# Norms of the Hyena filters: one channel per partition, and a later place for row 0

## The chip, the cores and the metric

The kernel runs on one core of a Trainium2 chip. The metric is the time of one execution on the device in microseconds (us), as the median of several runs. A core has five engines that work side by side, each through its own queue in order: TensorE (PE: matmuls; PEld is its loading of weights), VectorE (DVE), ScalarE (ACT), GpSimd (POOL) and SyncE (SP), which here only issues transfers.

## The reference, cut to what matters

One encoder block on x of shape (1, 2048, 1024): a projection, a Fourier group and a Hyena group side by side, an output projection, and an MLP. The change lies in the long filters of the Hyena group: 2 orders x 512 channels, each 4096 positions long.

```python
h = (h @ w_out).reshape(l, HYENA_ORDER, N_DIRECTIONS, HYENA_WIDTH)
h = h * decay[:, None, None, :]
k = concatenate([h_fwd[:1] + h_bwd[:1], h_fwd[1:], zeros, h_bwd[1:][::-1]], axis=0)
k = k * rsqrt(sum(k * k, axis=0, keepdims=True) + EPS)      # a norm for every channel
...
k_freq = rfft(k, axis=0)
for n, gate in enumerate((x1, x2)):
    z = gate * (irfft(rfft(z, 2l) * k_freq[:, n])[:l] + z * long_d[n])
```

## The kernel before, in words

The stages follow each other: first projection (two passes), Fourier group with the filters running beside it, rest of the filters, Hyena convolutions, output projection, MLP. The filters are the function `filters`. It works on eight units: `Unit(ct, n)` is a block of 128 channels (`ct` 0 to 3) of one order (`n` 0 or 1); units 0 to 3 are order 0, units 4 to 7 order 1.

A unit goes through these steps:

- `generate(q)`, q = 0 to 7: four matmuls make filter values (positions on partitions), DVE multiplies by a decay that was loaded (L500), ACT rounds to the high part (L181), DVE (even q) or POOL (odd q) subtracts for the low part (L182). For the norm ACT squares (L510) and POOL adds up over q (L511); after q = 7 two more additions (L513, L514) leave one 128 x 128 tile of sums, positions by channels. The squares have a single buffer, so each waits for the addition before it.
- `normalise()`: a matmul of ones with this tile (L518) puts the sum of every channel into all 128 rows. DVE adds EPS, ACT takes the root, DVE the reciprocal and a Newton step (L197 to L208), all on 128 x 128. The filter itself stays unnormalised; the product of the two orders' norms scales v later (L534, L538). So that the skip term `z * long_d` comes out right, long_d divided by the norm is added to the filter's position 0: `dk` is loaded, multiplied and added to the saved row 0 (L526 to L528) on one partition, and rounded and subtracted into row 0 of the high and low parts (L531, L532).
- `stage1(c)`, c = 0 to 7: three matmuls with 512 columns each (high x high, high x low, low x high: L189 to L191), then a DVE transpose into `Gk` (L418). Row 0 is among what it reads, in both parts.
- `stage2(q)`, q = 0 to 7: four matmuls (L553) that read all eight transposes, a copy by ACT (L556), and after every second one a store by SP (L558).

The loop over units runs both stages of unit i, and generates unit i + 2 between them: at the steps of `GENERATE` (3, 5, 7, 7, 9, 11, 13, 15, where steps 0 to 7 are stage 1 and 8 to 15 stage 2). Unit i + 1 is normalised in unit i's second stage, behind q = 1 (in unit 0: behind c = 5 of the first stage). Unit 0 is normalised while unit 1 is generated, beside the Fourier group. In unit 6 the first stage of unit 7 is put between the last steps of the second stage (`LAST`).

The order in every engine's queue is made when the program is built. Program order is the priority; a planner keeps its own clock for each operation, and where the operand of the next one isn't there yet by that clock it puts other, ready work in front. On the chip each queue then runs as laid down. Semaphores and waits are placed by the same framework. Buffers rotate in pools; the results of matmuls take eight banks in turn.

Of the kernel before, what the change touches and what calls it, by code (L numbers as in the profile page):

```python
# [10 lines left out]
F32 = mybir.dt.float32  # L11
# [3 lines left out]
ALU = mybir.AluOpType  # L15

EPS = 1e-5
# [110 lines left out]
P = 128  # L128
# [6 lines left out]
def hybrid_block(ctx: ExitStack, tc: tile.TileContext, A, out):  # L135
    nc = tc.nc
# [25 lines left out]
    def pool(name, side="left"):  # L162
        return tc.tile_pool(name=name, bufs=1, side=side, reuse_waits="tile")

    def pa(nm):
        return ps.tile([P, 512], F32, tag="a", name=nm, bufs=8)
# [304 lines left out]
    def filters(ctx, fp, gp, zp, zzs, norms, emb, wo, e1k, f2):  # L471


        e1h, e1l = (fp.tile([P, P], FR, tag=n, name=n) for n in ("e1h", "e1l"))
        split(e1h, e1l, e1k)

        class Unit:
            def __init__(self, ct, n):
                self.ct, self.n = ct, n

            def generate(self, q):
                if q == 0:

                    i = units.index(self)
                    if i in (1, 4):
                        k = zp.tile([P, 2, 8, 32, 16], FR, tag="zz", name="k")
                        self.k = [k[:, j] for j in range(2)]
                    else:
                        self.k = [(sp if i in (2, 5, 7) else fp).tile([P, 8, 32, 16], FR, tag=n, name=n) for n in ("kh", "kl")]
                    self.acc = fp.tile([P, 4, 128], F32, tag="acc", name="acc", bufs=2)  # L490
                if q % 2 == 0:
                    self.dec = load(fp, "dec", [P, 8, 128], A["decay"][self.ct][:, 4 * q : 4 * q + 8, :], 2)
                dec = self.dec[:, 4 * (q % 2) : 4 * (q % 2) + 4, :]
                p = pa("pk")
                for i in range(4):
                    nc.tensor.matmul(
                        p[:, 128 * i : 128 * i + 128], lhsT=emb[:, 4 * q + i, :], rhs=wo[:, self.n, 128 * self.ct : 128 * self.ct + 128], start=True, stop=True
                    )
                k4 = fp.tile([P, 4, 128], F32, tag="kt", name="kt", bufs=2)
                nc.vector.tensor_mul(k4, p.rearrange("p (l c) -> p l c", l=4), dec)  # L500
                if q == 0:
                    self.k0 = fp.tile([1, 128], F32, tag="k0", name="k0", bufs=2)
                    nc.vector.tensor_copy(self.k0, k4[0:1, 0, :])
                hi, lo = (t.rearrange("p c l j -> p l c j")[:, 4 * q : 4 * q + 4] for t in self.k)
                split(hi, lo, k4.rearrange("p l (c j) -> p l c j", c=8), None, nc.gpsimd if q % 2 else nc.vector)
                if q == 0:
                    nc.scalar.square(self.acc, k4)
                else:
                    sq = fp.tile([P, 4, 128], F32, tag="sqr", name="sqr")
                    nc.scalar.square(sq, k4)  # L510
                    nc.gpsimd.tensor_add(self.acc, self.acc, sq)  # L511
                if q == 7:
                    nc.gpsimd.tensor_add(self.acc[:, 0:2, :], self.acc[:, 0:2, :], self.acc[:, 2:4, :])  # L513
                    nc.gpsimd.tensor_add(self.acc[:, 0, :], self.acc[:, 0, :], self.acc[:, 1, :])  # L514

            def normalise(self):
                p = pa("psum_k")
                nc.tensor.matmul(p[:, 0:128], lhsT=ones, rhs=self.acc[:, 0, :], start=True, stop=True)  # L518
                v = fp.tile([P, 128], F32, tag="vk", name="vk")
                nc.vector.tensor_scalar(out=v, in0=p[:, 0:128], scalar1=EPS, scalar2=None, op0=ALU.add)  # L520
                sc = rsqrt(v, fp, "k")
                nc.vector.tensor_copy(norms[:, self.n, self.ct], sc)

                dk = fp.tile([1, 128], F32, tag="dk", name="dk")
                nc.sync.dma_start(dk, A["long_d"][:, 2 * self.ct + self.n, :])
                nc.vector.tensor_mul(dk, dk, v[0:1, :])  # L526
                nc.vector.tensor_mul(dk, dk, sc[0:1, :])
                nc.vector.tensor_add(dk, dk, self.k0)  # L528
                hi, lo = (t[0:1, :, 0, :] for t in self.k)
                k0 = dk.rearrange("p (c j) -> p c j", c=8)  # L530
                nc.vector.tensor_copy(hi, k0)  # L531
                nc.vector.tensor_sub(lo, k0, hi)  # L532
                if self is units[7]:
                    nc.gpsimd.tensor_mul(norms[:, 0], norms[:, 0], norms[:, 1])  # L534

            def scale(self, q, eng):
                z = zzs[0][:, 4 * q : 4 * q + 4, 128 * self.ct : 128 * self.ct + 128]
                eng.tensor_mul(z, z, norms[:, 0, self.ct : self.ct + 1, :].broadcast_to([P, 4, 128]))  # L538

            def stage1(self, c):  # L540
                if c == 0 and self is units[7]:

                    self.G = fp.tile([P, 64, 32, 2], F32, tag="kh", name="Gk")
                elif c == 0:
                    self.G = gp.tile([P, 64, 32, 2], F32, tag="Gk", name="Gk")
                p = pa("pk1")
                mm3(p, e1h, e1l, self.k[0][:, c], self.k[1][:, c], True, True)
                turned(self.G, c, p.rearrange("p (l c e) -> p c e l", c=8, e=2))

            def stage2(self, q):  # L550
                p = pa("pk2")
                for j in range(4):
                    nc.tensor.matmul(p[:, 128 * j : 128 * j + 128], lhsT=f2[:, 4 * q + j, :], rhs=self.G[:, :, 4 * q + j], start=True, stop=True)  # L553
                if q % 2 == 0:
                    self.ks = sp.tile([P, 8, 128], F32, tag="ks", name="ks", bufs=3)
                nc.scalar.copy(self.ks[:, 4 * (q % 2) : 4 * (q % 2) + 4, :], p.rearrange("p (f c) -> p f c", f=4))  # L556
                if q % 2:
                    nc.sync.dma_start(kd[self.ct][self.n][:, 4 * q - 4 : 4 * q + 4, :], self.ks)  # L558

        units = [Unit(ct, n) for n in range(2) for ct in range(4)]  # L560
        for u in units[:2]:
            for q in range(8):
                u.generate(q)
                if u is units[1] and q == 3:
                    units[0].normalise()
                yield
        sp = ctx.enter_context(pool("spectra", "right"))

        GENERATE = [(3, 5, 7, 7, 9, 11, 13, 15)] * 5 + [(7, 7, 8, 9, 10, 11, 12, 13)]

        LAST = ((), (), (), (), (), (0, 1, 2), (3, 4, 5), (6, 7))
        for i, u in enumerate(units):
            new = units[i + 1] if i < 7 else None

            def generate(step):
                for q in range(8 if i < 6 else 0):
                    if GENERATE[i][q] == step:
                        units[i + 2].generate(q)

            for c in range(8 if new else 0):  # L580
                u.stage1(c)
                if i == 0 and c == 5:
                    new.normalise()
                generate(c)
            for q in range(8):
                u.stage2(q)
                if i == 6:
                    for c in LAST[q]:
                        new.stage1(c)
                if i and new and q == 1:  # L590
                    new.normalise()
                generate(8 + q)
                if q % 4 == 0 and i > 4:
                    ct = 2 * i - 11 + q // 4
                    if 0 <= ct < 4:
                        cs = slice(128 * ct, 128 * ct + 128)
                        if ct == 0:
                            zzs.append(zp.tile([P, NT, 512], F32, tag="zz", name="zz"))
                        nc.sync.dma_start(zzs[0][:, :, cs], gd[0][:, :, cs])
                j = 8 * i + q - 50  # L600
                if 0 <= j < 8:
                    units[j // 2].scale(2 * (j % 2), nc.gpsimd)
                    units[j // 2].scale(2 * (j % 2) + 1, nc.vector)
# [630 lines left out]
    with pool("ip") as ip, pool("cp1") as cp1:  # L1234
# [52 lines left out]

        run(project(ip, fx, (None, cp1), (-1, 0), uf), tables())
        e1f, e1k, turn, gy, e1z, wo, emb, f2 = got
    norms = early.enter_context(pool("norms", "right")).tile([P, 2, 4, 128], F32, tag="norms", name="norms")  # L1290
    with pool("filters") as fp:
        zzs = []
        gp = early.enter_context(pool("gk", "right"))
# [83 lines left out]
```

## Time and profile before

| | |
|---|---|
| median of 3 runs | 2336.13 us (2333.21 to 2342.69) |
| the profiled execution | 2342.11 us |
| its span, first to last instruction | 2340.2 us |
| TensorE busy, mean granted clock | 2247.7 us (96%), 0.986 |
| VectorE, ScalarE, GpSimd busy | 1548.4, 1104.3, 846.8 us |
| first `generate` matmul | 422.1 us |
| first `stage1` of unit 0 | 467.5 us |
| first matmul of the Hyena stage | 643.8 us |
| bytes moved | 468.41 MB, 200 GB/s in the mean |

Lines of a group in the profile read: line of the code, engine, operation, output <- inputs, shapes, count | busy us and mean ns of one | idle time of the engine just before them, and what ended most of it. Lines of a timeline read: start in us, duration, engine, line, operation, count of merged instructions, and in brackets the idle time ahead and what ended it. A matmul of 32-bit operands shows as two passes (x8 for the four of a step). Matmuls overlap, so their durations add up to more than they take; the distance from one start to the next is what one costs.

### The profile page before, as it was taken

Reading aid. Unit: us, or ns where it says so; the run is one execution under the profiler, and the core shown is the slowest. Engines: PE = TensorE matmul, PEld = TensorE weight load, DVE = VectorE, ACT = ScalarE, POOL = GpSimd, SP = SyncE. Lnnn points to the kernel's source line nnn. Section 1 sums busy time; section 2 is a strip of 40 time slices with the busy share of each in tenths; the row PEclk is TensorE's granted clock in tenths of the full one; section 3 lists DMA queues with packets and bytes.
Section 4 is the critical chain, followed back from the end, with each engine's and each line's share of the span. In section 5 each row is a group of like instructions: output and inputs, shape, how many; then the busy total and the mean of one; then the engine's idle time right before and its main releaser. Section 6 shows DMA issues by size and latency. Waiting matters only on the chain.

```text
span 2340.2 us, 30973 instructions
## 1 busy us (share of the span) xinstructions
PE 2247.7 (96%) x10984; PEld 1861.0 (80%) x10984; DVE 1548.4 (66%) x2284; ACT 1104.3 (47%) x1809; POOL 846.8 (36%) x634
## 2 busy tenths in 40 slices
PE   8999998989899989998999999999999999999998
PEld 6887787788788857886788877888888888888886
DVE  7998666789767874447544456444466666866667
ACT  6554211455455554545655566555543333533334
POOL 4345322566656622216755565555400000000000
PEclk9999999999999989999999999999999999999999
DMA  7535888456688986557544456444479766866631
GB/s 258 178 134 179 304 321 300 139 174 206 227 207 191 212 224 189 176 175 244 162 150 149 152 207 203 153 149 151 151 261 377 238 197 196 280 209 197 192 123 72
DMA packets 294779, 468.41 MB, mean 200 GB/s; under 512 B 18453, under 2 KB 142687, under 8 KB 290273
## 3 DMA queue, kind: packets, MB, share of 16 engines
q1 hardware_dynamic: 291265, 460.43, 61.5%
q10 hardware_dynamic: 3360, 6.02, 0.8%
q8 instruction: 86, 1.41, 0.3%
q14 instruction: 68, 0.56, 0.1%
HBM read 312.54 MB, written 152.27 MB: 199 GB/s over the span
## 4 chain that ended last, share of the span: by engine, by line
PE 73%; DMA 9%; DVE 9%; ACT 3%; POOL 3%; issue 2%; SPq 1%; ACTq 0%; DVEq 0%; POOLq 0%
PE p2u L190 5%; PE p2u L189 5%; PE p2u L191 5%; PE p1u L191 5%; PE p1u L189 5%; PE p1u L190 4%; DMA ks<-spec 3%; PE pu L191 3%; PE pu L190 3%; PE pu L189 3%; PE p2v L189 2%; PE p2v L190 2%; PE p2v L191 2%; DMA f<-in_w_fc 2%; PE p1v L189 2%; PE p1v L191 2%
## 5 line engine op out<-in xcount | busy, mean ns | idle before, releaser
L181 ACT CAST qahm<-ra 128x1024 fp32r<-128x1024 f32 x110 | 115.9, 1053 | 345.9 <-PE p2u L190 172.0
L182 DVE TENSOR_TENSOR qalm<-ra,qahm 128x1024 fp32r<-128x1024 f32 x110 | 134.7, 1225 | 155.5 <-ACT qahm L181 151.8
L1159 POOL TENSOR_TENSOR acc<-acc,gfin 128x512 f32<-128x512 f32 x4 | 5.1, 1279 | 633.1 <-DMA out<-acc 625.9
L189 PE MATMUL pu<-wh,xh 128*128 128x512 f32 x512 | 205.7, 403 | 8.9 <-ACT wh L184 5.5
L190 PE MATMUL pu<-wl,xh 128*128 128x512 f32 x512 | 202.6, 396 | 6.5 <-DVE wl L182 3.7
L191 PE MATMUL pu<-wh,xl 128*128 128x512 f32 x512 | 203.0, 397 | 2.7 <-DVE xl L182 2.7
L190 PE MATMUL p2u<-qblm,qahm 128*128 128x512 f32 x504 | 196.2, 389 | 0.5 <-DVE qblm L182 0.5
L189 PE MATMUL p2u<-qbhm,qahm 128*128 128x512 f32 x504 | 195.9, 389 | 0.1
L191 PE MATMUL p2u<-qbhm,qalm 128*128 128x512 f32 x504 | 195.8, 389 | 0.0
L182 DVE TENSOR_TENSOR qblm<-rb,qbhm 128x1024 fp32r<-128x1024 f32 x110 | 134.1, 1219 | 1.4 <-ACT qbhm L181 1.1
L397 POOL TENSOR_TENSOR acc<-acc,cw 128x512 f32<-128x512 f32 x45 | 60.8, 1351 | 202.8 <-DVE acc L374 201.4
L189 PEld LDWEIGHTS pu<-wh,xh 128*128 128x128 f32 x512 | 98.1, 192 | 31.1 <-ACT wh L184 7.0
L181 ACT CAST ahm<-s 128x512 fp32r<-128x512 f32 x124 | 76.6, 620 | 95.3 <-PE p1v L190 55.2
L190 PEld LDWEIGHTS pu<-wl,xh 128*128 128x128 f32 x512 | 98.0, 191 | 28.9 <-DVE wl L182 4.1
L182 POOL TENSOR_TENSOR alm<-W,ahm 128x512 fp32r<-128x512 f32 x63 | 85.9, 1364 | 94.2 <-ACT ahm L181 94.2
L181 ACT CAST qbhm<-rb 128x1024 fp32r<-128x1024 f32 x110 | 115.3, 1049 | 5.0 <-DMA a1m<-c 2.9
L191 PEld LDWEIGHTS pu<-wh,xl 128*128 128x128 f32 x512 | 97.8, 191 | 24.1 <-DVE xl L182 3.6
L189 PEld LDWEIGHTS p2u<-qbhm,qahm 128*128 128x128 f32 x504 | 94.5, 188 | 20.6 <-ACT qbhm L181 0.5
L190 PEld LDWEIGHTS p2u<-qblm,qahm 128*128 128x128 f32 x504 | 94.6, 188 | 20.3 <-DVE qblm L182 1.0
L191 PEld LDWEIGHTS p2u<-qbhm,qalm 128*128 128x128 f32 x504 | 94.6, 188 | 19.8
L191 PE MATMUL p1u<-bm,alm 128*128 128x512 f32 x252 | 100.1, 397 | 6.4 <-DVE alm L182 6.4
L189 PE MATMUL p1u<-bm,ahm 128*128 128x512 f32 x252 | 100.2, 397 | 6.2 <-ACT ku L1022 6.2
(380 smaller groups left out, 6445.4 us busy)
## 6 DMA issues: line engine op xcount, KB each, us to landing
W<-in_w_fc SPq DMA_DIRECT2D x66, 512.0 KB, 4.4
ks<-spec SPq DMA_DIRECT2D x128, 256.0 KB, 6.8
rb<-td SPq DMA_DIRECT2D x64, 512.0 KB, 4.5
ra<-a1m SPq DMA_DIRECT2D x56, 512.0 KB
ra<-a0m SPq DMA_DIRECT2D x54, 512.0 KB, 10.7
rb<-in_w_fc SPq DMA_DIRECT2D x46, 512.0 KB, 4.5
f<-in_w_fc SPq DMA_DIRECT2D x16, 1024.0 KB
td<-f SPq DMA_DIRECT2D x16, 1024.0 KB, 5.0
```

What stands on the lines that cost most here:

```text
L181: nc.scalar.copy(hi, src)
L182: (eng or nc.vector).tensor_sub(lo, src, hi)
L189: nc.tensor.matmul(o, lhsT=lh, rhs=rh, start=start, stop=False, skip_group_check=more)
L190: nc.tensor.matmul(o, lhsT=lh, rhs=rl, start=False, stop=False, skip_group_check=more)
L191: nc.tensor.matmul(o, lhsT=ll, rhs=rh, start=False, stop=stop, skip_group_check=more)
L397: nc.gpsimd.tensor_add(m1, m1, cw[:, 3, :])
L1159: nc.gpsimd.tensor_mul(acc[i][:, c], acc[i][:, c], gfin[:, c])
```

## The change

- `normalise` turns the matmul round: the tile of sums is the stationary operand, one column of ones the moving one, so the sums come out as [128, 1], a channel on each partition. EPS, root, reciprocal and Newton step work on [128, 1]; the Newton step takes the branch for one column in `rsqrt`. `dk` is long_d times variance times inverse root, also [128, 1].
- long_d is loaded once at the start for all units (two loads), turned by a PE transpose and kept as [128, 8].
- A new step `skip` brings `dk` back to a row: a matmul of `dk` with the identity, and a second that adds the saved row 0. ACT rounds row 0 into the high part from PSUM, DVE subtracts for the low part.
- For order 1 the product of both orders' inverse norms is put on a diagonal (ACT) in `normalise`, and `skip` multiplies ones with it, which gives the product in every row; ACT copies it to `norms`. The POOL product of all norms goes.
- `normalise` of unit i + 1 is called behind c = 2 of the first stage, `skip` behind q = 0 of the second. For unit 0 they are called behind q = 2 and q = 6 of unit 1's generation.

```diff
@@ filters @@
+        longd = fp.tile([P, 8], F32, tag="longd", name="longd")
+        rows = fp.tile([8, 128], F32, tag="dk8", name="dk8")
+        for n in range(2):
+            nc.sync.dma_start(rows[4 * n : 4 * n + 4, :], A["long_d"].rearrange("a (c n) j -> n (a c) j", n=2)[n])
+        p = pa("plongd")
+        nc.tensor.transpose(p[:, 0:8], rows, ident[0:8, 0:8])
+        nc.scalar.copy(longd, p[:, 0:8])
...
             def normalise(self):
+                i = units.index(self)
                 p = pa("psum_k")
-                nc.tensor.matmul(p[:, 0:128], lhsT=ones, rhs=self.acc[:, 0, :], start=True, stop=True)
-                v = fp.tile([P, 128], F32, tag="vk", name="vk")
-                nc.vector.tensor_scalar(out=v, in0=p[:, 0:128], scalar1=EPS, scalar2=None, op0=ALU.add)
-                sc = rsqrt(v, fp, "k")
-                nc.vector.tensor_copy(norms[:, self.n, self.ct], sc)
-
-                dk = fp.tile([1, 128], F32, tag="dk", name="dk")
-                nc.sync.dma_start(dk, A["long_d"][:, 2 * self.ct + self.n, :])
-                nc.vector.tensor_mul(dk, dk, v[0:1, :])
-                nc.vector.tensor_mul(dk, dk, sc[0:1, :])
-                nc.vector.tensor_add(dk, dk, self.k0)
+                nc.tensor.matmul(p[:, 0:1], lhsT=self.acc[:, 0, :], rhs=ones[:, 0:1], start=True, stop=True)
+                v = fp.tile([P, 1], F32, tag="vk", name="vk", bufs=2)
+                nc.vector.tensor_scalar(out=v, in0=p[:, 0:1], scalar1=EPS, scalar2=None, op0=ALU.add)
+                self.sc = rsqrt(v, fp, "k", 8)
+                self.dk = fp.tile([P, 1], F32, tag="dk", name="dk", bufs=2)
+                nc.vector.tensor_scalar(out=self.dk, in0=v, scalar1=self.sc, scalar2=longd[:, i : i + 1], op0=ALU.mult, op1=ALU.mult)
+                if self.n:
+                    both = fp.tile([P, 1], F32, tag="both", name="both", bufs=2)
+                    nc.vector.tensor_scalar(out=both, in0=self.sc, scalar1=units[i - 4].sc, scalar2=None, op0=ALU.mult)
+                    self.diag = fp.tile([P, 128], F32, tag="diag", name="diag")
+                    nc.scalar.mul(self.diag, ident, both)
+
+            def skip(self):
+                p = pa("pdk")[0:1, 0:128]
+                nc.tensor.matmul(p, lhsT=self.dk, rhs=ident, start=True, stop=False)
+                nc.tensor.matmul(p, lhsT=ones[0:1, 0:1], rhs=self.k0, start=False, stop=True)
                 hi, lo = (t[0:1, :, 0, :] for t in self.k)
-                k0 = dk.rearrange("p (c j) -> p c j", c=8)
-                nc.vector.tensor_copy(hi, k0)
+                k0 = p.rearrange("p (c j) -> p c j", c=8)
+                nc.scalar.copy(hi, k0)
                 nc.vector.tensor_sub(lo, k0, hi)
-                if self is units[7]:
-                    nc.gpsimd.tensor_mul(norms[:, 0], norms[:, 0], norms[:, 1])
+                if self.n:
+                    p = pa("pdiag")
+                    nc.tensor.matmul(p[:, 0:128], lhsT=ones, rhs=self.diag, start=True, stop=True)
+                    nc.scalar.copy(norms[:, self.ct], p[:, 0:128])
...
-                if u is units[1] and q == 3:
+                if u is units[1] and q == 2:
                     units[0].normalise()
+                if u is units[1] and q == 6:
+                    units[0].skip()
...
                 u.stage1(c)
-                if i == 0 and c == 5:
+                if c == 2:
                     new.normalise()
                 generate(c)
             for q in range(8):
                 u.stage2(q)
...
-                if i and new and q == 1:
-                    new.normalise()
+                if new and q == 0:
+                    new.skip()
```

`norms` becomes [128, 4, 128] instead of [128, 2, 4, 128], and `scale` reads it so.

More of the change, by code (lines that the diff above doesn't have):

```diff
@@ L532, in normalise @@
                 nc.vector.tensor_sub(lo, k0, hi)
-                if self is units[7]:
-                    nc.gpsimd.tensor_mul(norms[:, 0], norms[:, 0], norms[:, 1])
+                if self.n:
+                    p = pa("pdiag")
+                    nc.tensor.matmul(p[:, 0:128], lhsT=ones, rhs=self.diag, start=True, stop=True)
+                    nc.scalar.copy(norms[:, self.ct], p[:, 0:128])
             def scale(self, q, eng):
                 z = zzs[0][:, 4 * q : 4 * q + 4, 128 * self.ct : 128 * self.ct + 128]
-                eng.tensor_mul(z, z, norms[:, 0, self.ct : self.ct + 1, :].broadcast_to([P, 4, 128]))
+                eng.tensor_mul(z, z, norms[:, self.ct : self.ct + 1, :].broadcast_to([P, 4, 128]))
@@ L1289, in hybrid_block @@
         e1f, e1k, turn, gy, e1z, wo, emb, f2 = got
-    norms = early.enter_context(pool("norms", "right")).tile([P, 2, 4, 128], F32, tag="norms", name="norms")
+    norms = early.enter_context(pool("norms", "right")).tile([P, 4, 128], F32, tag="norms", name="norms")
     with pool("filters") as fp:
```

## The prediction

> **What bounds the kernel now.** I read the page first, then the windows, the chain, and last each engine's rows inside the filter stage.
>
> ```profile
> PE 2247.7 (96%) x10984; PEld 1861.0 (80%) x10984; DVE 1548.4 (66%) x2284; ACT 1104.3 (47%) x1809; POOL 846.8 (36%) x634
> ```
>
> TensorE (PE) is busy for 96% of the whole span, so a change to the filters can pay only where PE waits inside them. The windows below begin at unit 0's first spectrum matmul (467.4 us) and end where the Hyena stage starts (643.9); they are cut at each unit's first one. Columns: length, busy time and count of PE, weight loads, VectorE (DVE), ScalarE (ACT), GpSimd (POOL), then granted clock, DMA share, GB/s.
>
> ```profile
> 467.40:643.90 176.50, 156.02 (x1106) 142.57 (x1106) 149.51 (x240) 92.25 (x179) 115.15 (x93) 0.97 0.60 203
> ```
> ```profile
> 467.40:482.60 15.20, 9.91 (x61) 8.36 (x60) 13.25 (x25) 6.09 (x18) 9.64 (x8) 1.00 0.48 160
> 482.60:495.00 12.40, 12.34 (x95) 12.34 (x96) 8.37 (x15) 9.08 (x18) 8.21 (x7) 0.86 0.55 186
> 495.00:516.90 21.90, 20.86 (x158) 19.30 (x156) 20.05 (x32) 11.81 (x23) 14.96 (x13) 1.00 0.54 189
> 516.90:539.80 22.90, 20.88 (x154) 19.17 (x154) 21.09 (x35) 13.27 (x25) 15.71 (x13) 1.00 0.53 186
> 539.80:562.70 22.90, 20.84 (x154) 19.19 (x154) 21.09 (x35) 13.26 (x25) 15.68 (x13) 1.00 0.53 185
> 562.70:585.60 22.90, 20.88 (x154) 19.18 (x154) 21.09 (x34) 13.26 (x25) 15.71 (x13) 1.00 0.72 230
> 585.60:609.90 24.30, 20.86 (x154) 19.17 (x154) 19.59 (x33) 14.12 (x27) 15.79 (x13) 1.00 0.97 294
> 609.90:626.20 16.30, 12.96 (x73) 11.05 (x74) 12.39 (x23) 6.09 (x11) 8.09 (x8) 0.90 0.69 260
> 626.20:643.90 17.70, 16.49 (x105) 14.82 (x106) 12.60 (x17) 5.28 (x9) 11.37 (x7) 0.90 0.26 102
> ```
>
> PE idles 176.50 - 156.02 = 20.5 us here. The clock adds a second loss: 0.86, 0.90 and 0.90 in three windows, or 12.4 x 0.14 + 16.3 x 0.10 + 17.7 x 0.10 = 5.1 us. In a steady window DVE has 21.09 of 22.90 us, more than PE. Who ends the idle time on PE (last columns), and the chain that ends one steady window:
>
> ```profile
> L553 PE MATMUL pk<-Gk,f 128*128 128x128 f32 x512 | 64.6, 277 | 7.0 <-DVE Gk L418 7.0
> L190 PE MATMUL pk<-kl,e1h 128*128 128x512 f32 x48 | 20.8, 433 | 2.9 <-DVE kl L532 2.9
> L189 PE MATMUL pk<-kh,e1h 128*128 128x512 f32 x48 | 20.2, 428 | 6.9 <-DVE kh L531 4.2 <-ACT ks L556 2.7
> L518 PE MATMUL psum_k<-acc,ones 128*128 128x128 f32 x14 | 2.8, 280 | 2.2 <-POOL acc L514 2.2
> ```
> ```profile
> 556.97 1.39 DVE nw_k L206
> 558.52 0.68 DVE kt L500
> 559.89 0.29 DVE dk L528
> 560.20 1.19 DVE k L531
> 561.41 1.27 DVE k L532
> 562.73 0.50 PE pk L190
> ```
>
> The reader sees the norm's elementwise chain run on DVE up to the last instant, write row 0 of the filter (L531, L532), and release the next unit's first spectrum matmul. The 7.0 us behind L418 are transposes queued on DVE behind the same chain.
>
> **The change part by part.**
>
> *DVE.* What goes, in whole-stage sums:
>
> ```profile
> L198 DVE RECIPROCAL rc_k<-sq_k 128x128 f32<-128x128 f32 x8 | 7.6, 952 | 3.6 <-ACT sq_k L197 3.5
> L526 DVE TENSOR_TENSOR dk<-dk,vk 1x128 f32<-1x128 f32 x8 | 7.5, 936 | 0.2
> L206 DVE TENSOR_TENSOR nw_k<-nw_k,vk 128x128 f32<-128x128 f32 x8 | 7.5, 934 | 0.2
> L532 DVE TENSOR_TENSOR kl<-dk,kh 1x128 fp32r<-1x128 f32 x6 | 6.4, 1059 | 0.1
> L531 DVE CAST kh<-dk 1x128 fp32r<-1x128 f32 x6 | 6.3, 1045 | 0.1
> L207 DVE TENSOR_SCALAR nw_k<-nw_k 128x128 f32<-128x128 f32 x8 | 1.8, 220 | 0.2
> ```
>
> The first five alone are 35.3 us over eight units. The [128,1] forms that replace them stand elsewhere in this trace:
>
> ```profile
> L203 DVE TENSOR_SCALAR nw_s<-nw_s,rc_s 128x1 f32<-128x1 f32 x80 | 15.8, 210 | 1.0
> L202 DVE TENSOR_SCALAR nw_s<-nw_s 128x1 f32<-128x1 f32 x80 | 11.7, 150 | 1.0
> ```
> ```profile
> L526 DVE TENSOR_TENSOR dk<-dk,vk x8: 273/1260/1381, 456.8 to 620.5; 1x128 f32<-1x128 f32 x8
> ```
>
> (The last row is shortest, median and longest of L526, in ns.) Per unit: variance, reciprocal, three Newton steps, dk and, in half the units, both: six or seven at 0.15 to 0.21 each, about 1.2 us, plus the subtraction into lo. That one is a 1x128 two-input operation: 0.27 if undisturbed as in L526's shortest case, 1.06 if disturbed as L532 is in the mean; I take 0.3, because one of its inputs now is PSUM, and only the other is in the memory that POOL uses too. So some 1.5 us replace at least 4.4 per unit (35.3/8), and DVE falls to about 18 of 22.9: PE leads again. I do not credit this as time; it pays only through PE's waits.
>
> *TensorE.* The norm matmul keeps its two passes. Its price is the gap between its start and the next matmul's:
>
> ```profile
> 551.55 0.38 PE L518 MATMUL psum_k<-acc,ones 128*128 128x128 f32 x2
> 551.77 1.06 PE L496 MATMUL pk<-wo,emb 128*128 128x128 f32 x8
> ```
>
> 0.22 us for 128 columns. New are two such matmuls in skip (0.44) and a third in units 4 to 7 (0.22): 7 x 0.44 + 4 x 0.22 = 4.0 us inside the windows. A one-row lhsT may load faster, down to nothing, or not at all faster; 0.44 is the upper end and I take it. One transpose for longd costs another 0.22 at the start and a possible wait on its load; the first fetch in PE's queue is far ahead of its use, so zero, up to 2 us if PE meets it early.
>
> *ACT.* The square root shrinks, and three small operations come in (row 0, the diagonal, the norms). ACT has 13.3 of 22.9 us; even at 1 us each they fit into the 9.6 that are free, so zero. If ACT stands behind a sum that is late, the row-0 copy is late with it: priced under the rivals.
>
> *POOL and SP.* One 1.3 us product of norms goes; the scaling of v no longer waits for all eight units. Eight small loads leave SP's queue and two replace them; those eight waited on L532, with stores behind them, but no PE wait names those stores, so I value this at zero, and it costs nothing if that fails.
>
> *The move.* The norm matmul goes from two steps into the second stage to three steps into the first; row 0 is written after the first second-stage step, with seven second-stage and four generate steps ahead of its reader, some 11 us by L553's 64.6 us for 64 steps. So the waits on L531 and L532 go. What is late next is the sum itself:
>
> ```profile
> 494.23 1.05 PE L496 MATMUL pk<-wo,emb 128*128 128x128 f32 x8
> ```
> ```profile
> 496.98 0.40 PE L191 MATMUL pk<-k,e1l 128*128 128x512 f32 x1
> ```
> ```profile
> 504.28 1.95 PE L553 MATMUL pk<-Gk,f 128*128 128x128 f32 x16
> ```
> ```profile
> 500.25 0.46 POOL L514 TENSOR_TENSOR acc<-acc 128x128 f32<-128x128 f32 x1
> ```
>
> The unit's last generate matmul starts at 494.23; the third stage-1 group (the new place of the norm matmul) ends at 497.2; POOL's last sum ends at 500.7. At its written place PE would stand 3.5 us. But the queue's order is planned, and the plan lets ready work pass:
>
> ```profile
> 626.21 0.93 PE L189 MATMUL pk<-kh,e1h 128*128 128x512 f32 x3 [2.49 <-DVE kh L531]
> 626.97 0.45 PE L553 MATMUL pk<-Gk,f 128*128 128x128 f32 x2
> 627.11 0.74 PE L190 MATMUL pk<-kl,e1h 128*128 128x512 f32 x1
> ```
>
> In the code each L189 is followed by its L190 and L191; here three L189 and part of stage 2 were placed in front because kl was planned late. So I expect the norm matmul two or three groups later, with the plan off by something: 0 to 3.5 us, I take 0.5, since only stage-1 and generate steps have to move up and both are ready.
>
> **The sum**, by windows (ceiling: all idle and slow clock gone, less new work):
> - 467.4 to 495: idle 5.35, clock 1.7, new 0.4. The 2.2 us on POOL stay (its chain is untouched), half a microsecond of L418 stays: 3.9.
> - 495 to 585.6: idle 7.1, new 2.0, four leftovers of 0.5: 3.1.
> - 585.6 to 626.2: idle 6.8, clock 1.6, new 1.3: ceiling 7.1. But unit 7's sums hang on decay loads:
>
> ```profile
> 603.43 0.69 DVE L500 TENSOR_TENSOR kt<-pk,dec 128x512 f32<-128x512 f32 x1 [2.96 <-PE pk L553]
> ```
>   The stop before this row ends with the decay load that the chain names there, while the window's DMA share is 0.97; that does not get faster. I leave 2.1 for it: 5.0.
> - 626.2 to 643.9: idle 1.2, clock 1.8; I leave 0.8 for transposes: 2.2.
>
> Together 14.2 us. Bounds: 20.5 + 5.1 - 4.0 = 21.6 us gained; below, the rivals. Everything later starts off the Hyena stage's first matmul, so I pass it on whole. The profiled execution took 2342.1 us (span 2340.2), 6.0 above the median 2336.1; I take the gain off the median: 2322.
>
> [...]
>
> **Rivals.**
> 1. *The norm matmul stays where it is written* (slower). Each steady unit then loses 3.5 and gains 1.8 - 0.5: -2.2 x 4 = -8.8; before 495 and from 585.6 to 626.2 nothing is gained, since the same wait eats it; the tail's 2.2 remains: 2336.1 + 6.6 = 2343. For it: the matmul did stand 2.2 us on L514 once already. Against it: the reordered rows. It decides from about 2.8 us of mean wait per unit.
> 2. *The small operations are stretched by POOL* (slower). L531 takes 1.05 us in the mean for one row. If all seven [128,1] steps took that, the chain would be 7.3 us; between the sum's end (500.7) and skip's place (behind the first of the two second-stage steps that begin at 504.28, so 505.2) there are 4.5. PE would stand about 3.5 us in each of seven units (with the square root between): 24 more than forecast, 2346. Against it: L207, the same kind of operation at the same time, keeps 0.22. It decides from a chain of about 6.5 us.
>    [...]
> 3. *Half of it comes back.* Row 0's waits go, but in-order queues on ACT and DVE make new ones of 1 us a unit, and DMA holds unit 7: gain 6, 2330. For it: ACT's square stands on POOL's sums in every unit.
> 4. *All waits go*: 2315.
>
> **How the numbers follow.** Forecast 0.55 (its own range 2316 to 2329), rival 3 0.22, rival 4 0.12, rival 1 0.07, rival 2 0.04. Half a percent, 11.7 us, is what a measurement of this kernel can tell from no change: faster means below 2324.4. Two thirds of the forecast's chance lies there (0.38) and all of rival 4: 0.50. Slower means above 2347.8: half of rivals 1 and 2, 0.05. The rest is 0.45. The range 2313 to 2337 takes in the forecast and rivals 3 and 4 and leaves out the slower ones.
>
> **What would show it.** Right: no PE wait named after row 0; DVE at about 18 us in a steady window; units 22 us or less apart; clock 1.00 behind 610 us; the norm matmul behind the fifth or sixth stage-1 group. Wrong: PE idle before the norm matmul of over 2 us a unit (rival 1), [128,1] operations above 0.5 us (rival 2), or PE idle before skip's matmul (3).

## The result, and the profile after

The changed kernel takes 2366.92 us (median of 4 runs, 2366.64 to 2378.55) where the kernel before took 2339.41 beside it: a ratio of 1.013 [1.0086, 1.0173]. It is 1.3% slower, clear of the noise; the forecast was 2322. The profiled execution took 2366.64 us with a span of 2364.8.

All of it lies between unit 0's first spectrum matmul and the Hyena stage's first matmul. That stretch was 643.8 - 467.5 = 176.3 us and is now 668.5 - 467.8 = 200.7. What follows it lasts as long as before: 2340.2 - 643.8 = 1696.4 and 2364.8 - 668.5 = 1696.3.

The page's engine line of the changed kernel, then its windows, cut like those of before at each unit's first spectrum matmul (length, busy time and count of PE, weight loads, DVE, ACT, POOL, then granted clock as a share of full TensorE speed, DMA share, GB/s):

```profile
PE 2263.4 (96%) x11025; PEld 1869.2 (79%) x11025; DVE 1511.9 (64%) x2248; ACT 1108.7 (47%) x1826; POOL 839.9 (36%) x633
```
```profile
467.70:668.50 200.80, 170.23 (x1141) 151.46 (x1141) 113.28 (x206) 94.72 (x187) 107.26 (x90) 0.90 0.52 175
467.70:491.20 23.50, 21.19 (x160) 19.21 (x160) 15.20 (x30) 13.09 (x28) 13.79 (x12) 1.00 0.50 161
491.20:517.30 26.10, 22.76 (x161) 20.47 (x160) 14.97 (x29) 14.09 (x29) 15.36 (x14) 0.93 0.52 179
517.30:544.60 27.30, 23.98 (x160) 21.52 (x159) 14.95 (x28) 13.52 (x27) 14.98 (x14) 0.87 0.46 154
544.60:572.20 27.60, 24.27 (x163) 21.82 (x163) 15.06 (x29) 14.16 (x30) 15.10 (x14) 0.88 0.44 150
572.20:599.60 27.40, 24.08 (x162) 21.68 (x161) 17.00 (x30) 11.71 (x25) 16.29 (x14) 0.88 0.54 183
599.60:628.10 28.50, 23.02 (x162) 20.68 (x162) 18.45 (x32) 12.25 (x25) 19.42 (x16) 0.88 0.79 229
628.10:652.80 24.70, 16.04 (x82) 12.62 (x82) 12.01 (x22) 9.99 (x20) 12.31 (x11) 0.79 0.46 169
652.80:668.50 15.70, 14.89 (x107) 13.45 (x106) 5.65 (x8) 5.92 (x11) 0.00 (x0) 1.00 0.43 171
```

Set against the windows of before, in order: -4.1 us for the first (23.5 against 15.2 + 12.4), then +4.2, +4.4, +4.7, +4.5, then +4.2 and +8.4, and -2.0 for the last: +24.3. PE's idle time grew from 20.5 to 30.6 us, its busy time from 156.0 to 170.2. DVE fell from 149.5 to 113.3.

Two more views of the stage: all waits of PE that it names (total, times, longest), and, in unit 1's window, the way of unit 2's sum from POOL to PE, with the matmuls behind it.

```profile
PE psum_k L528 <- POOL acc L522: 28.8, 7, 7.7
PE pk L572 <- DVE Gk L418: 1.6, 2, 0.8
PE pk L189 <- ACT ks L575: 0.2, 1, 0.2
```
```profile
494.26 1.26 POOL L519 TENSOR_TENSOR acc<-acc,sqr 128x512 f32<-128x512 f32 x1
495.60 0.72 POOL L521 TENSOR_TENSOR acc<-acc 128x256 f32<-128x256 f32 x1
496.40 0.45 POOL L522 TENSOR_TENSOR acc<-acc 128x128 f32<-128x128 f32 x1
```
```profile
496.91 0.38 PE L528 MATMUL psum_k<-ones,acc 128*128 128x1 f32 x2 [3.33 <-POOL acc L522]
497.16 0.48 PE L189 MATMUL pk<-k,e1h 128*128 128x512 f32 x1
...
500.03 0.63 PE L191 MATMUL pk<-k,e1l 128*128 128x512 f32 x1
500.46 0.63 PE L189 MATMUL pk<-k,e1h 128*128 128x512 f32 x1
500.89 0.63 PE L190 MATMUL pk<-k,e1h 128*128 128x512 f32 x1
...
502.93 0.39 PE L190 MATMUL pk<-k,e1h 128*128 128x512 f32 x1
503.15 0.39 PE L191 MATMUL pk<-k,e1l 128*128 128x512 f32 x1
```

The waits on row 0 are gone, those on L418 fell from 7.0 to 1.6, and one wait has taken their place: the norm matmul (now L528) stands 28.8 us on the last POOL sum (now L522), once in every unit from 1 to 7. A stand is time in which PE waits with the next instruction of its queue. (The title's "later place for row 0" means later than the norm. Against the kernel before, row 0 of units 2 to 7 is written one second-stage step earlier, behind q = 0 and not q = 1.)

The stand itself is only a part of the price. Behind the one shown, the same matmuls start 0.43 us apart (500.03, 500.46, 500.89) where they otherwise start 0.22 to 0.23 apart (502.93, 503.15): PE falls to about half its speed for some 3 us, and the window's granted clock is 0.93. In the next three units the norm matmul itself is already slow (0.58 to 0.59 us for 0.38) and the slow stretch lasts some 6 us, from 577.88 to 583.6 for example; those windows have 0.87 and 0.88. The slow matmuls show as busy time, not as idle time. That is why busy PE grew by 14 us, more than the added matmuls take (6.5 us, worked out below).

### The profile page after: what moved, and what is told of

The parts are those of the page before. It is cut to its first block, busy times and chain, and to the rows that moved or that the text cites. A ratio compares the mean times of both kernels' runs of the same rounds, so it can differ in the third digit from the quotient of the medians.

```text
span 2364.8 us, 31017 instructions
## 1 busy us (share of the span) xinstructions
PE 2263.4 (96%) x11025; PEld 1869.2 (79%) x11025; DVE 1511.9 (64%) x2248; ACT 1108.7 (47%) x1826; POOL 839.9 (36%) x633
## 5 line engine op out<-in xcount | busy, mean ns | idle before, releaser
L182 DVE TENSOR_TENSOR qalm<-ra,qahm 128x1024 fp32r<-128x1024 f32 x110 | 134.7, 1224 | 154.6 <-ACT qahm L181 151.7
L189 PE MATMUL pu<-wh,xh 128*128 128x512 f32 x512 | 206.4, 404 | 4.3 <-ACT wh L184 3.8
L189 PE MATMUL p2u<-qbhm,qahm 128*128 128x512 f32 x504 | 195.9, 389 | 0.0
L182 DVE TENSOR_TENSOR qblm<-rb,qbhm 128x1024 fp32r<-128x1024 f32 x110 | 134.0, 1218 | 1.1 <-ACT qbhm L181 1.1
L189 PEld LDWEIGHTS pu<-wh,xh 128*128 128x128 f32 x512 | 98.4, 192 | 26.1 <-ACT wh L184 4.9
L182 POOL TENSOR_TENSOR alm<-W,ahm 128x512 fp32r<-128x512 f32 x63 | 84.6, 1344 | 95.0 <-ACT ahm L181 95.0
L190 PEld LDWEIGHTS p2u<-qblm,qahm 128*128 128x128 f32 x504 | 94.6, 188 | 20.2 <-DVE qblm L182 0.6
L189 PEld LDWEIGHTS p2u<-qbhm,qahm 128*128 128x128 f32 x504 | 94.6, 188 | 20.2 <-issue 0.3
L189 PE MATMUL p1u<-bm,ahm 128*128 128x512 f32 x252 | 100.2, 398 | 8.2 <-ACT ku L1043 7.2
```

What stands on the lines that cost most here:

```text
L182: (eng or nc.vector).tensor_sub(lo, src, hi)
L189: nc.tensor.matmul(o, lhsT=lh, rhs=rh, start=start, stop=False, skip_group_check=more)
L190: nc.tensor.matmul(o, lhsT=lh, rhs=rl, start=False, stop=False, skip_group_check=more)
```

## The experiments

Two theories stood at the start. *Place*: the norm matmul waits where it is written, for a sum that POOL ends later, and the slow clock follows from the stand; the new form of the arithmetic is harmless or good. *Form*: the [128, 1] steps, the skip matmuls or the diagonal cost the time. The stage, as above from unit 0's first L189 to the first Hyena matmul, is the measure, read from one profiled execution of each kernel. What comes after it lasts 1692 to 1703 us: 1696.4 before, longest behind the two shortest stages (1702.5 in form_only, 1699.6 in late) and shortest behind the longest (1692.1 in sum_pre). So a part of what the stage gains can be lost again later; more on this at late.

| kernel | stage, us | stands before the norm matmul, steady units | median, us | ratio to before |
|---|---|---|---|---|
| before | 176.3 | 0 (2.2 once, in unit 0) | 2339.2 and 2337.6 | 1 |
| the change | 200.7 | 3.3 | 2366.92 | 1.013 [1.0086, 1.0173] |
| sum_c5 | 179.9 | 0.4 | 2352.2 | 1.0066 [1.004, 1.0091] |
| form_only | 165.4 | 0 | 2333.06 | 0.9979 [0.9967, 0.9991] |
| move_only | 196.5 | 3.9 | 2360.9 | 1.0098 [1.0072, 1.0124] |
| filled | 189.7 | 0.6 and 12 matmuls | 2356.9 | 1.008 [1.0061, 1.01] |
| sum_pre | 211.4 | 5.4 | 2381.73 | 1.0185 [1.016, 1.021] |
| sum_on_pe | 193.1 | 2.0 | 2358.13 | 1.0077 [1.0059, 1.0095] |
| late | 165.2 | 0 | 2329.71 | 0.9969 [0.9958, 0.998] |

**sum_c5**: the norm matmul three stage-1 groups later.

```diff
-                if c == 2:
+                if c == 5:
                     new.normalise()
```

> The changed kernel with one edit: the norm matmul is called behind c = 5 instead of c = 2. Theory A (PE stands in front of the norm matmul until POOL's last sum is there, and its clock falls behind each stand): the sum comes 6.4 us after the unit's last generate matmul; three more groups and one generate step lie ahead, so the stand falls from 3.3 to about 0.6 us in four units, from 2.3 to 0 in the first, from 5.5 to 3.4 and 7.7 to 5.6 in the last two; granted clock 1.00 in the steady windows; steady windows 21.5 to 22 us instead of 27.4; time about 2338 us. Theory B (the [128,1] form and its extra matmuls cost the time, wherever they stand): no change, 2365.

PE's wait on the sum in the stage:

```profile
PE psum_k L528 <- POOL acc L522: 11.2, 6, 6.3
```

28.8 became 11.2, and 20.8 us of the stage's 24.4 came back: more than the 17.6 us of stands that went, because the clock came back too (0.94 over the stage, 0.90 in the change). This is from a good execution: the profiled one, 2345.28 us, was the fastest of four, which reach 2356.16. By the medians 14.7 of 27.5 us came back, and 2352.2 misses the 2338 that had been expected. What is left of the wait is 0.4 us in the steady units, 6.27 and 3.28 in the last two units. That is the part of the stage where the trace of before had decay loads late (DMA share 0.97), and the change stands longest there too (5.48 and 7.66); that the loads are the cause was not tried, and the scaling of v, below, is another candidate. So the place decides, and for the last units even c = 5 is too early.

**form_only** and **move_only**: the two halves by themselves. The first has the new arithmetic with the norm matmul at its old place and skip behind the fifth second-stage step; the second has the old 128 x 128 arithmetic, skip included, called at the new place.

```diff
 form_only, against the changed kernel
-                if c == 2:
+                if i == 0 and c == 5:
                     new.normalise()
...
-                if new and q == 0:
+                if i and new and q == 1:
+                    new.normalise()
+                if new and q == 4:
                     new.skip()
```
```diff
 move_only, against the kernel before
-                if i == 0 and c == 5:
+                if c == 2:
                     new.normalise()
...
-                if i and new and q == 1:
-                    new.normalise()
```

> The changed kernel's form at the old place: norm matmul behind q = 1 of the second stage (unit 1: behind c = 5), skip behind q = 4. Theory A: no stand of PE in front of the norm matmul but the 2 us in unit 1, no wait for row 0 (written some 4.5 us of PE work ahead of its reader); about 2322 us, between 2315 and 2330. Theory B: as slow as the changed kernel, 2360 or more.

> The kernel before with the place alone changed: its 128 x 128 norm and its one-row skip chain on DVE, called behind c = 2. Theory A: PE stands 3.3 us in front of the norm matmul as in the changed kernel, the clock falls too, and DVE is as full as before, so 2365 to 2380 us. Theory B: about as before, 2340, since only the place changed; less if the wait for row 0 goes.

For form_only the stage's window, and the waits of PE in it:

```profile
466.00:631.40 165.40, 157.52 (x1142) 143.38 (x1141) 114.06 (x206) 93.12 (x187) 109.17 (x90) 0.98 0.63 213
```
```profile
PE pk L572 <- DVE Gk L418: 5.2, 3, 2.4
PE pdiag L552 <- ACT diag L539: 1.8, 3, 0.8
PE pdk L544 <- DVE dk L533: 0.9, 4, 0.2
```

For move_only PE's wait on the sum (L518 and L514 are the lines of before):

```profile
PE psum_k L518 <- POOL acc L514: 31.2, 7, 5.3
```

The form alone takes 10.9 us off the stage, the move alone adds 20.2. Both together add 24.4, not 9.3: the two are not additive, since most of the waits that the form takes away (on DVE's long chain) are gone from the moved kernel anyway. In move_only PE has no wait on L531 or L532, and 3.3 us on L418 for 7.0. The theory that the form costs the time has fallen. Neither time was met: form_only's median of 2333.06 lies above the 2315 to 2330 that had been expected, move_only's 2360.9 below 2365 to 2380. The change is 4.2 us slower than the move alone though its stands are 2.4 us shorter. The matmuls that the form adds, 6.5 us (worked out below), are about the sum of the two; the waits on L418 differ too (1.6 for 3.3), and no run took the matmuls away, so this is not shown.

**filled**: the changed kernel with twelve matmuls, whose result nothing reads, put ahead of each norm matmul of units 1 to 7, so that PE works through most of the stand.

```diff
+                if i:
+                    f = pa("fill")
+                    for c in range(12):
+                        nc.tensor.matmul(f, lhsT=e1h, rhs=units[i - 1].k[0][:, c % 8], start=True, stop=True)
                 nc.tensor.matmul(p[:, 0:1], lhsT=self.acc[:, 0, :], rhs=ones[:, 0:1], start=True, stop=True)
```

> The changed kernel with twelve matmuls of 512 columns (2.8 us at full clock, their result is not read) placed in PE's queue just ahead of the norm matmul, where PE would stand. The sum is not earlier. Theory A with its clock part: the stand is filled, the clock stays at 1.00 in the steady windows, which shrink from 27.4 to about 24.7 us; about 12 us less in all, 2354. If the clock is no part of it: 2367, windows as they are. Theory B: 2367 or more, since PE gets work.

The timeline of PE round the norm matmul that stood 3.33 us above:

```profile
493.95 2.96 PE L530 MATMUL fill<-k,e1h 128*128 128x512 f32 x12
497.51 0.38 PE L532 MATMUL psum_k<-ones,acc 128*128 128x1 f32 x2 [0.60 <-POOL acc L522]
497.76 0.48 PE L189 MATMUL pk<-k,e1h 128*128 128x512 f32 x1
...
499.66 0.39 PE L190 MATMUL pk<-k,e1h 128*128 128x512 f32 x1
499.89 0.39 PE L191 MATMUL pk<-k,e1l 128*128 128x512 f32 x1
500.12 0.40 PE L189 MATMUL pk<-k,e1h 128*128 128x512 f32 x1
```

The sum comes when it came before (stand and filler together are 3.4 us), and yet the stage is 11.0 us shorter: the matmuls behind run 0.23 us apart at once, and the stage's granted clock is 0.97 for 0.90. The norm matmuls of the steady units follow each other at 24.6 to 24.8 us, where they came at 26.1 to 27.5. Work that computes nothing made the kernel faster, and the median of 2356.9 is near the 2354 that had been expected. So of the change's 24.4 us, at least 11 are the slow clock behind the stands: the fillers took it away and left the sum where it was. (The last two units still stand 2.89 and 4.53 us.)

**sum_pre**: normalise called ahead of the loop over c, three groups earlier still. If a queue's order could let ready work pass, this would hardly differ from the change.

```diff
+            if new:
+                new.normalise()
             for c in range(8):
                 u.stage1(c)
-                if c == 2:
-                    new.normalise()
```

> The changed kernel with the norm matmul called ahead of the first stage-1 group, directly behind the unit's last generate matmul; nothing else moved. If the planner lets ready matmuls pass a matmul whose sum is late by its own clock (what the prediction assumed, with a clock that is some 3 us too early), it stands again behind the third group or later, and stands and time are those of the changed kernel (3.3 us, 2367). If PE's queue keeps program order here, it stands ahead of the first group, PE stands 5.4 us in each of four units instead of 3.3 and the clock falls each time; the filter stage from the first stage-1 group to the first Hyena matmul grows from 200.7 to 210 to 216 us, time 2376 to 2383.

PE's timeline at the same unit, then the order of PE's work there in the traces of the two kernels:

```profile
499.56 0.59 PE L528 MATMUL psum_k<-ones,acc 128*128 128x1 f32 x2 [5.39 <-POOL acc L522]
500.01 0.77 PE L189 MATMUL pk<-k,e1h 128*128 128x512 f32 x1
```
```
 the change                        sum_pre
 L189, L190, L191  (c = 0)         L528 psum_k
 L189, L190, L191  (c = 1)         L189, L190, L191  (c = 0)
 L189, L190, L191  (c = 2)         L189, L190, L191  (c = 1)
 L528 psum_k                       L189, L190, L191  (c = 2)
```

The matmul stands exactly where it is written, and PE with it, 5.4 us in a steady unit and 10.41 in the last; the stage is 211.4 us and the median 2381.73, both as expected for a queue that keeps program order. (The ratio is from two runs.) Nothing passes it: in the stand shown, PE waits 5.39 us with three ready groups behind.

**sum_on_pe**: the last two POOL additions go, and the norm matmul adds up the four tiles itself, four matmuls for one.

```diff
-                    nc.gpsimd.tensor_add(self.acc[:, 0:2, :], self.acc[:, 0:2, :], self.acc[:, 2:4, :])
-                    nc.gpsimd.tensor_add(self.acc[:, 0, :], self.acc[:, 0, :], self.acc[:, 1, :])
...
-                nc.tensor.matmul(p[:, 0:1], lhsT=self.acc[:, 0, :], rhs=ones[:, 0:1], start=True, stop=True)
+                for j in range(4):
+                    nc.tensor.matmul(p[:, 0:1], lhsT=self.acc[:, j, :], rhs=ones[:, 0:1], start=j == 0, stop=j == 3)
```

> The changed kernel, still behind c = 2, but POOL's last two additions (1.2 us) go: PE adds the four slices itself, with four one-column matmuls into the same bank. The chain of the sum is 1.3 us shorter, 0.45 us of PE work more. Theory A: stands of 3.3 fall to about 2.0 us; if a stand of 2.0 is too short to bring the clock down (the first unit's 2.3 us was followed by full clock), the clock stays at 1.00 in the steady windows and each loses 1.3 + 2.7 - 0.45 = 3.5 us; stage 200.7 to about 184, time about 2350. If the clock falls anyway: 1 us a unit, 2361. Theory B (the form costs): 2367 or more.

The norm matmuls of four units, and the windows from each unit's first spectrum matmul that hold them:

```profile
495.33 1.05 PE L528 MATMUL psum_k<-ones,acc 128*128 128x1 f32 x8 [2.00 <-POOL acc L519]
520.75 1.05 PE L528 MATMUL psum_k<-ones,acc 128*128 128x1 f32 x8 [1.99 <-POOL acc L519]
544.60 1.87 PE L528 MATMUL psum_k<-ones,acc 128*128 128x1 f32 x8 [1.99 <-POOL acc L519]
571.79 1.86 PE L528 MATMUL psum_k<-ones,acc 128*128 128x1 f32 x8 [1.99 <-POOL acc L519]
```
```profile
491.00:516.40 25.40, 23.40 (x167) 21.21 (x166) 14.75 (x29) 14.19 (x29) 14.17 (x12) 0.93 0.54 183
516.40:540.20 23.80, 21.81 (x166) 19.81 (x165) 14.62 (x28) 13.61 (x27) 13.67 (x12) 1.00 0.51 172
540.20:567.00 26.80, 24.81 (x165) 22.47 (x165) 14.71 (x29) 13.71 (x29) 13.73 (x11) 0.87 0.45 157
567.00:594.00 27.00, 25.01 (x167) 22.66 (x166) 17.37 (x31) 11.47 (x24) 15.12 (x11) 0.87 0.57 191
```

The stands shrink by the 1.3 us that POOL no longer needs, as expected. The clock is where this kernel teaches most: four stands of the same 2.0 us, and the clock is 1.00 behind one of them, 0.93 behind another and 0.87 behind two. The unit is 23.8 us long where the clock holds and 26.8 to 27.0 where it doesn't: 3.0 to 3.2 us for the clock alone, more than the stand costs. So shortening the stand to 2 us doesn't keep the clock in every unit. The median, 2358.13, lies between the two times that had been expected, 2350 with the clock kept and 2361 with it lost.

**late**: the new form with the norm matmul just behind the first second-stage step (q = 1 for the last, unit 1 still behind c = 5) and skip behind q = 4; the version to which the others point.

```diff
-                if c == 2:
+                if i == 0 and c == 5:
                     new.normalise()
...
-                if new and q == 0:
+                if i and new and q == (1 if i == 6 else 0):
+                    new.normalise()
+                if new and q == 4:
                     new.skip()
```

> The [128,1] form with the norm matmul behind q = 0 of the second stage (unit 1: c = 5 of the first; unit 7: q = 1), skip behind q = 4. Against the same form with the matmul behind q = 1, the diagonal and dk get two PE steps more: the waits of 0.2 us on dk and of 0.5 to 0.8 us on the diagonal go, some 3 us in the stage (165.4 to about 162.5). Theory A: no stand in front of the norm matmul, since the sum comes 6.4 us behind the last generate matmul and this place is 10 us behind it; clock as in that run; time 2330, faster than the kernel before by 0.3 to 0.5%.

The stage, a steady unit, and all the waits of PE in it:

```profile
471.10:636.30 165.20, 157.29 (x1141) 142.99 (x1140) 115.16 (x205) 92.67 (x187) 108.60 (x90) 0.98 0.64 213
513.00:534.20 21.20, 21.00 (x160) 19.27 (x160) 15.70 (x28) 13.28 (x27) 15.10 (x14) 1.00 0.60 205
```
```profile
PE pk L572 <- DVE Gk L418: 6.1, 3, 3.3
PE pdiag L552 <- ACT diag L539: 1.0, 2, 0.5
PE pdk L544 <- DVE dk L533: 0.8, 4, 0.2
```

No norm matmul waits, PE is busy for 21.0 of a steady unit's 21.2 us, and the stage is 11.1 us shorter than before. The time is 0.9969 [0.9958, 0.998] of the kernel before: some 0.3% faster, with the median at the 2330 that had been expected. The interval overlaps form_only's, so no order of the two is shown. The stage is no shorter than form_only's (165.2 and 165.4), and not the 162.5 that had been expected: the waits on dk and the diagonal, which were to go, are still 0.8 and 1.0 us, and the one on L418 rose by 0.9. Of these two places behind the sum, one is as good as the other.

The medians give 7.9 us of the stage's 11.1, and 6.2 of form_only's 10.9. The profiles show where a part of the rest is lost (late's was the longest of its eleven executions, 2337.66). From its first matmul to the first one of the output projection the Hyena stage lasts 243.5 us in late and 243.1 in form_only for 239.6 before, and PE's waits there on DVE's y are 14.8 and 14.1 us for 10.2. Why was not tried.

## Why the prediction was wrong

- **The step that failed: "the plan lets ready work pass".** From one place of the trace, at 626.21, where three L189 and a part of stage 2 had been put in front of the readers of a late kl, the prediction concluded that the norm matmul would slide two or three groups back, and wrote 0.5 us for each leftover. The wait measured 3.3 us in the steady units, 5.48 and 7.66 in the last two. sum_pre shows the rule that held here: the matmul stays where it is written. The prediction's own figure for that case, 3.5 us "at its written place", was right to 0.2 us; it was then argued away. Why row 0's readers were reordered in the kernel before and the norm matmul not is not settled; no run tried it. A planner whose own clock has the sum ready too early by more than these stands would look the same.
- **Rival 1 was what happened**, and its sign (PE idle before the norm matmul over 2 us a unit) showed it, but it was given 0.07 and 2343. Its size was off by two terms. The slow clock behind a stand, at least 11 us by filled, was left out: the rival priced idle time only. And it said that "from 585.6 to 626.2 nothing is gained", where the stands of 5.48 and 7.66 us in the last units made +4.2 and +8.4. It also set the point of decision at 2.8 us of mean wait. With the clock in the sum it lies lower: sum_on_pe waits 19.1 / 7 = 2.7 us in the mean and its stage is 16.8 us longer than before; sum_c5 waits 11.2 / 7 = 1.6 and its stage is 3.6 us longer.
- **A term put at zero came back in the last units.** That "the scaling of v no longer waits for all eight units" was valued at nothing. In the kernel before, the scaling starts at 624.7. In the change its first steps (L557) lie in the queues ahead of unit 6's sum: DVE waits 3.10 us for the load of v until 592.68 and goes on with the decay (L508) only at 595.66; POOL scales for 3.40 us from 593.48. How much of the 5.48 us this makes was not tried.
- **The gains were right where the wait didn't eat them.** The first window gave 4.1 (predicted 3.9), the last 2.0 (2.2), with its clock back from 0.90 to 1.00. Between them 3.1 + 5.0 was predicted and -17.8 - 12.6 came. With the matmul moved behind its sum, form_only and late have 10.9 and 11.1 us of the 14.2. "I pass it on whole" held for the change, whose time behind the stage is that of before; it did not hold for these two, whose medians keep 6.2 and 7.9 us.
- **DVE right in direction, too small.** The five rows and their substitutes promised 8 x (4.4 - 1.5) = 23 us; the stage's DVE time fell by 36.2. Rows of the old chain had gone uncounted, L528 (3.6), L205 (3.0) and two units' L531 and L532 (5.0) among them.
- **Rival 2 is excluded, but not by the changed kernel itself:** there POOL has nothing to do while the chain runs, from 496.85 to 504.38 in unit 1's window. In late it is at work beside the chain, and the two timelines show what that does to it:

```profile
504.79 1.30 POOL L182 TENSOR_TENSOR kl<-kt,kh 128x512 fp32r<-128x512 f32 x1
506.04 1.27 POOL L519 TENSOR_TENSOR acc<-acc,sqr 128x512 f32<-128x512 f32 x1
```
```profile
505.81 0.27 DVE L201 TENSOR_SCALAR nw_k<-rc_k,vk 128x1 f32<-128x1 f32 x1
506.12 0.15 DVE L202 TENSOR_SCALAR nw_k<-nw_k 128x1 f32<-128x1 f32 x1
506.31 0.21 DVE L203 TENSOR_SCALAR nw_k<-nw_k,rc_k 128x1 f32<-128x1 f32 x1
506.61 1.25 DVE L182 TENSOR_TENSOR kl<-kt,kh 128x512 fp32r<-128x512 f32 x1
```

  The [128, 1] operations keep 0.15 to 0.27 us; the large subtraction L182 behind them, with two inputs, takes 1.25 beside POOL; in the change it took 0.65 at 501.34, where POOL was idle. The subtraction into lo (L549 of the changed kernel, one input in PSUM), priced at 0.3, took 0.27 to 0.28 us in units 1 to 7, in five of them with POOL at work all through it; L532 of the kernel before, with both inputs in SBUF, had a median of 1.26.
- **TensorE's new work was priced too low.** 4.0 us were predicted, with 0.44 for skip's two matmuls as "the upper end". The prediction's own measure, the distance of starts, gives more in the change:

```profile
479.79 1.06 PE L572 MATMUL pk<-Gk,f 128*128 128x128 f32 x8
480.78 0.38 PE L544 MATMUL pdk<-ident,dk 128*1 128x128 f32 x2
481.09 0.37 PE L545 MATMUL pdk<-k,ones 1*1 1x128 f32 x2
481.39 1.16 PE L572 MATMUL pk<-Gk,f 128*128 128x128 f32 x8
```

  The two take 0.31 and 0.30 us, and the second-stage steps on both sides take longer for being parted: from 479.79 to the next group at 482.39 are 2.60 us, where two such steps without skip take 1.79 (483.28 to 485.07). So skip costs 0.81 us, and 1.03 with the diagonal (2.82 from 587.99 to 590.81): 3 x 0.81 + 4 x 1.03 = 6.5 us. (The windows of the prediction's sum hold 0.4 + 2.0 + 1.3 = 3.7 of its 4.0.) That late's steady unit still gains 22.9 - 21.2 = 1.7 us, about the 2.0 of idle time less 0.44, is luck. With 0.81 for skip, the waits of before must have cost some 2.5 us in such a unit, an estimate from these figures and more than their idle time.
- **ACT and SP at nothing: right in the change.** No wait of PE in its stage names the loads or a store, and the one on ACT is 0.2 us. In form_only and late the diagonal, made by ACT, costs 1.8 and 1.0 us. Rival 3's sign, PE idle before skip's matmul, is absent in the change.
- **The clock was weighed the wrong way.** In the kernel before, 2.49 us of idle time ahead of 626.21 went with a window of 0.90. The prediction counted this slow clock as 1.8 us to win back, and didn't ask what stands of 3.5 us, its own figure for the written place, would do to the clock. In the change stands of 3.3 us came with windows of 0.87 to 0.93. Some shorter ones did too: in sum_on_pe stands of 2.0 us lowered the clock in three units of four (0.93, 0.87, 0.87) and left it at 1.00 in the fourth, as unit 1's stand of 2.31 us, ahead of 472.41, did in the change. What decides between such stands is not shown.

## What to carry to other kernels

Before an instruction is moved ahead in an engine's queue, find the end of what it reads, and price the whole distance as a stand (in sum_pre PE stood 5.39 us with three ready groups behind); that a scheduler reordered something elsewhere is no evidence that it will do so here. Price a stand of TensorE at more than its length: here the unit behind a stand of 2.0 us lasted 23.8 us with the clock kept and 26.8 to 27.0 with it lost (sum_on_pe), 3.0 to 3.2 us more. The matmuls behind the stand then started 0.43 us apart and not 0.23, for 3 to 7 us in the units shown, and that hides in the busy time. Keep a wait that goes apart from the place to which the work goes: here the new form was worth 11 us of the stage with the norm matmul at its old place or just behind the end of its sum, and with that form the early place cost 35 (200.7 for 165.4).

## What the runs showed of the hardware

- Behind a stand of 1.99 us TensorE ran at about half its speed for some 6 us in two units and at its full speed in another, in one execution of one kernel (sum_on_pe: matmuls 0.43 us apart against 0.23, windows of 26.8 and 27.0 against 23.8 us). Twelve matmuls without use in the place of each stand took 11.0 us off the stage (filled, 189.7 for 200.7).
- The four norm matmuls at 544.60 took 1.87 us where the same four took 1.05 at 520.75: there the speed was down by the end of a 2 us stand, not only later. In the changed kernel's unit 1, in contrast, the first matmuls behind a 3.33 us stand (497.16 and on) still ran at full speed, and the slow ones came one to two microseconds later.
- DVE operations on [128, 1] kept 0.15 to 0.27 us beside a busy POOL (late, 505.62 to 506.52), where one-row operations of the kernel before had 1.05 and 1.06 us in the mean (L531, L532).
